# The inverse multiplied into the state's readers, the decay into its update rows, ahead of a recurrence's chain

## The chip, the cores and the metric

One core of a Trainium2 chip runs the whole program in one launch. The metric is the device time of that launch in microseconds, the median over several runs. Three runs of the kernel before took 2877.94, 2882.4 and 2890.2 us.

## The reference, cut to what matters

The program is two blocks of two layers each. The change is in the mixer of the first block, which runs twice (layer 0 with 512 tokens of output, layer 1 with 256). One of its branches is a recurrence over 512 tokens (8 chunks of 64), in 4 heads of 64 channels and 2 directions d, in float32:

```
def step(S, inp):                       # S: (G, H, dh, dh), one state per direction and head
    r_t, w_t, k_t, v_t, z_t, b_t = inp
    s_z = einsum('ghvk,ghk->ghv', S, z_t)
    S = S * w_t[:, :, None, :] + s_z[..., None] * b_t[:, :, None, :] + v_t[..., None] * k_t[:, :, None, :]
    return S, einsum('ghvk,ghk->ghv', S, r_t)
```

The other branches of the mixer, all of which the program interleaves with the recurrence, are a neighbourhood attention (q, k, v by projection, softmax, output), a 31-tap convolution, and the projection of a modulation vector.

## The kernel before, in words

The recurrence is computed chunk by chunk. Two heads share the 128 partitions (`halves`: rows o of one head, rows r of the other), `hp` counts the two pairs of heads, `u = (2d+hp)*8 + c` a chunk c of direction d. Its stages are generators: prep (p) makes ZR (slot 0 the readers of the state for s_z, slot 1 the readers for the output) and BK (the update rows b and k), both divided or multiplied by the running decay LAM; gram (g) makes the masked products S of BK with ZR for each chunk; inverse (i) inverts a unit triangular 64x64 matrix per chunk into TD, by a forward substitution on VectorE over 32x32 blocks (lines 681 to 698), four transposes TD and two TN (lines 704, 706) and two rounds of 32x32 products on TensorE (psinv); chain (c) carries the state PP through the chunks.

A chunk of the chain is three products one behind the other. First ZR[c,0] x PP plus S x UV (the v rows) into a bank, copied by VectorE to RH (line 802); then TD x RH, copied to the other half of UV (line 810); then BT x UV, to which PP is added and which is multiplied by the chunk's decay (lines 821 to 824). `ready(c+1)` prepares the next chunk inside the chain: it transposes the v rows (products with `cst`, vv and vr) and BK on TensorE, and ScalarE writes them as UV (line 776) and BT (line 785). The output product py (S x UV and ZR[c,1] x PP, alternating into one bank) is not needed by the next chunk; layer 1 makes it for the last four chunks alone.

The order of the stages is written out by hand in the strings SEQ (layer 0 `...ggggginNnniNNcactcccttat...`, layer 1 `...gggiiNnnncttcmmaa...`, with n and N the six projections of q, k, v, called near, psnap in the profile; a attention, t taps, m modulation); within it a list scheduler sets the order on each engine when the program is built. The strings are the same in both kernels. A float32 product leaves two MATMUL records in the profile, a product of the projections (fp32r) one. In a row `out<-in,in` the moving operand stands first.

Of the kernel before, what the change touches and what calls it, by code (L numbers as in the profile page):

```python
# [10 lines left out]
F32 = mybir.dt.float32  # L11
F32R = mybir.dt.float32r
I32 = mybir.dt.int32
AF = mybir.ActivationFunctionType
ALU = mybir.AluOpType
AX = mybir.AxisListType
PSUM = bass.MemoryType.PSUM
NOSYNC = mybir.DependencyInfo(mybir.DependencyClass.NoSync, mybir.DependencyReason.DATA)
# [122 lines left out]
class K:  # L141
    def __init__(self, tc, nc, A):
        self.tc, self.nc, self.A = tc, nc, A
        self.last = {}
        self.n = 0
        self.lab = ""

# [4 lines left out]

    def mm(self, out, lhsT, rhs, start, stop, chain=None, **kw):
        i = self.nc.tensor.matmul(out, lhsT, rhs, start=start, stop=stop, **kw)  # L154
        return self._chain(i, chain)

    def tp(self, out, in_, ident, chain=None):
# [302 lines left out]
    def mixer(self, l, x, b, X, M, need):  # L460

        tc, nc, A = self.tc, self.nc, self.A
# [96 lines left out]
        SS = ExitStack()  # L559
# [97 lines left out]
        def gram():  # L657
# [6 lines left out]
            for dh in range(4):  # L664
                for ab in range(2):
                    o = slice(64 * ab, 64 * ab + 64)
                    for c4 in range(2):
# [7 lines left out]
                                                self.gm[:, None, 128 * ab:128 * ab + 64 * z].to_broadcast([128, 4, 64 * z]), ALU.mult)  # L675
                        yield

        def inverse():

            with pool("PI", "right") as PI:  # L680
                Ad = PI.tile([128, 32, 32], F32, name=self.nm("Ad"), tag="Ad")
                Xi = PI.tile([128, 32, 32], F32, name=self.nm("Xi"))
                nc.sync.dma_start(Xi, A["cst"][:, C_X0:C_X0 + 1024].rearrange("p (a b) -> p a b", a=32))
                for g in range(4):
                    o, to = slice(32 * g, 32 * g + 32), 32 * (g % 2)
# [12 lines left out]
                        nc.vector.tensor_reduce(Xi[:, r, t:t + 1], w, AX.X, ALU.add)  # L698
                yield
                TN = PI.tile([128, 32, 32], F32, name=self.nm("TN"), tag="pd")  # L700
                Gs = PI.tile([128, 32, 32], F32, name=self.nm("Gs"), tag="Ad")
                for g in range(4):
                    o, to = slice(32 * g, 32 * g + 32), 32 * (g % 2)
                    nc.vector.transpose(TD[o, :, to:to + 32].rearrange("p u s -> p s u"), Xi[o].rearrange("p j s -> p s j"))
# [2 lines left out]
                for uh in range(2):  # L707
                    pg = self.ps((128, 16, 32))
                    for u in range(16):
                        for ab in range(2):  # L710
                            a, b = slice(64 * ab, 64 * ab + 32), slice(64 * ab + 32, 64 * ab + 64)
                            self.mm(pg[b, u], S[a, 1 - ab, uh * 16 + u, 32:64], TN[a, uh * 16 + u], True, True,
                                    tile_position=(64 * ab, 64 * ab + 32))
                    for ab in range(2):
                        b = slice(64 * ab + 32, 64 * ab + 64)
                        nc.scalar.copy(Gs[b, uh * 16:uh * 16 + 16], pg[b])
                    pt = self.ps((128, 16, 32))
                    for u in range(16):
                        for ab in range(2):
                            a, b = slice(64 * ab, 64 * ab + 32), slice(64 * ab + 32, 64 * ab + 64)  # L720
                            self.mm(pt[a, u], Gs[b, uh * 16 + u], TD[b, uh * 16 + u, 32:64], True, True,
                                    tile_position=(64 * ab + 32, 64 * ab))
                    for ab in range(2):
                        a = slice(64 * ab, 64 * ab + 32)
                        nc.scalar.copy(TD[a, uh * 16:uh * 16 + 16, 32:64], pt[a])
            yield

        def near():
# [32 lines left out]

        def chain():

            with pool("PC", "right", bufs=2) as PC:
                def ready(c):

                    UV = PC.tile([128, 2, 2, 2, 64], F32, tag="UV", name=self.nm("UV"))
                    pv = self.ps((128, 2, 2, 64), tag="x")
                    for d in range(2):
                        for hp in range(2):  # L770
                            for ab in range(2):
                                o = slice(64 * ab, 64 * ab + 64)
                                self.mm(pv[o, d, hp], (vr if d else vv)[o, hp, c * 64:c * 64 + 64], self.ident[o, o], True, True, chain=pv)
                    for ab in range(2):
                        o = slice(64 * ab, 64 * ab + 64)
                        nc.scalar.copy(UV[o, :, :, ab], pv[o])
                    if c == 7:
                        return UV, None
                    BT = PC.tile([128, 2, 2, 2, 64], F32, tag="BT", name=self.nm("BT"))
                    pb = self.ps((128, 2, 2, 128), tag="x")  # L780
                    for d in range(2):
                        for hp in range(2):
                            self.tp(pb[:, d, hp], BK[:, 2 * d + hp, c].rearrange("p a t -> p (a t)"), self.ident, chain=pb)
                    for ab in range(2):
                        nc.scalar.activation(BT[:, :, :, ab], pb[:, :, :, 64 * ab:64 * ab + 64], AF.Copy, scale=self.sg[:, ab:ab + 1])
                    return UV, BT

                halves = [(slice(64 * ab, 64 * ab + 64), slice(64 - 64 * ab, 128 - 64 * ab)) for ab in range(2)]
                PP = [None, None]
                UV, BT = ready(0)  # L790
                for c in range(8):
                    RH, Pn = [], [None, None]
                    for d in range(2):
                        pr = self.ps((128, 2, 64), tag=f"c{d}")
                        for hp in range(2):
                            u = (2 * d + hp) * 8 + c
                            for ab, (o, r) in enumerate(halves):
                                self.mm(pr[r, hp], S[o, ab, u, 0:64], UV[o, d, hp, ab], True, PP[d] is None, chain=pr)
                                if PP[d] is not None:
                                    self.mm(pr[r, hp], ZR[o, 2 * d + hp, c, 0], PP[d][o, hp], False, True, chain=pr)  # L800
                        RH.append(PC.tile([128, 2, 64], F32, tag=f"RH{d}", name=self.nm("RH")))
                        nc.vector.tensor_copy(RH[d], pr)
                    for d in range(2):
                        pu = self.ps((128, 2, 64), tag=f"c{d}")
                        for hp in range(2):
                            u = (2 * d + hp) * 8 + c
                            for ab, (o, r) in enumerate(halves):
                                self.mm(pu[r, hp], TD[r, u], RH[d][r, hp], True, True, chain=pu)
                        for ab, (o, r) in enumerate(halves):
                            nc.vector.tensor_copy(UV[r, d, :, ab], pu[r])  # L810
                    for d in range(2):
                        if c == 7:
                            break
                        pp = self.ps((128, 2, 64), tag=f"c{d}")
                        for hp in range(2):
                            for ab, (o, r) in enumerate(halves):
                                self.mm(pp[o, hp], BT[:, d, hp, ab], UV[:, d, hp, ab], True, True, chain=pp)
                        Pn[d] = PC.tile([128, 2, 64], F32, tag=f"PP{d}", name=self.nm("PP"))
                        lam = LAM[:, 2 * d:2 * d + 2, c, 64:65].to_broadcast([128, 2, 64])
                        if PP[d] is None:  # L820
                            nc.vector.tensor_tensor(Pn[d], pp, lam, ALU.mult)
                        else:
                            nc.vector.tensor_add(Pn[d], pp, PP[d])
                            nc.vector.tensor_tensor(Pn[d], Pn[d], lam, ALU.mult)
                    nxt = ready(c + 1) if c < 7 else None
                    if need or c >= 4:
                        py = self.ps((128, 2, 2, 64), tag="x")
                        for d in range(2):
                            for hp in range(2):
                                u = (2 * d + hp) * 8 + c  # L830
                                for ab, (o, r) in enumerate(halves):
                                    self.mm(py[o, d, hp], UV[:, d, hp, ab], S[:, ab, u, 64:128], True, PP[d] is None, chain=py)
                                    if PP[d] is not None:
                                        self.mm(py[o, d, hp], PP[d][o, hp], ZR[o, 2 * d + hp, c, 1], False, True, chain=py)
                        nc.scalar.copy(ZR[:, :, c, 1], py.rearrange("p d h t -> p (d h) t"))
                    PP = Pn
                    if nxt:
                        UV, BT = nxt
                        yield
            SS.close()  # L840

        def attend():
# [808 lines left out]
```

## Time and profile before

| | us |
|---|---|
| median of three runs | 2882.4 |
| the profiled run | 2886.99 |
| its span | 2885.2 |
| gram's end to chain's start, layer 0 | 169.8 to 260.4 |
| chain, layer 0 | 260.4 to 353 |
| gram's end to chain's start, layer 1 | 1009.1 to 1070.9 |
| chain, layer 1 | 1070.9 to 1154 |

The profile is of one execution. TensorE (PE) is busy for 95% of the span; its weight loads (PEld) run beside its products. The two mixers take some 90 to 445 us and 950 to 1200 us of the span; what lies behind them (feed-forward, experts, the second block) is not touched by the diff.

### The profile page before, as it was taken

The numbers are of one execution on the slowest core, as the hardware profiler recorded it, in microseconds if no ns is written. First come the engines' busy times: TensorE is split into PE (matmuls) and PEld (weight loads), VectorE is DVE, ScalarE is ACT, GpSimd is POOL, SyncE is SP. The second block draws the span as 40 slices with busy tenths as digits, with TensorE's granted clock in tenths as the row PEclk, the third lists the DMA queues.
The fourth block names the chain that finished last, engine by engine and source line by source line (L and its number), as shares of the span: only waits on it lengthen the run. The fifth ranks groups of instructions, "written<-read, shape, count | busy, mean of one in ns | idle before, by whom it ended". The sixth has DMA issues, their size and how long they took to land. (4 is left out here: it accounts for less than half of the span.)

```text
span 2885.2 us, 42860 instructions
## 1 busy us (share of the span) xinstructions
PE 2750.6 (95%) x17006; PEld 2257.8 (78%) x17006; DVE 1988.4 (69%) x2753; ACT 1468.3 (51%) x2032; POOL 348.5 (12%) x256
## 2 busy tenths in 40 slices
PE   6998999999998879999989999999999999999999
PEld 4677656778886766677867777778777889998999
DVE  4685474322225796488878888888889868856784
ACT  3313243322224332477757777767777646644563
POOL 1420012211001610100000000000000221301120
PEclk9898799999999998999999999999999999999999
DMA  6122155333333224579988999899989835553453
GB/s 227 51 74 74 52 150 193 96 123 94 97 99 105 81 88 140 173 293 352 319 321 325 322 353 344 328 338 362 337 325 349 307 114 175 183 183 117 161 184 109
DMA packets 108098, 585.77 MB, mean 203 GB/s; under 512 B 12657, under 2 KB 19825, under 8 KB 54129
## 3 DMA queue, kind: packets, MB, share of 16 engines
q1 hardware_dynamic: 107888, 582.95, 57.5%
q8 instruction: 136, 2.23, 0.3%
q14 instruction: 74, 0.60, 0.1%
HBM read 580.80 MB, written 2.10 MB: 202 GB/s over the span
## 5 line engine op out<-in xcount | busy, mean ns | idle before, releaser
L183 DVE TENSOR_TENSOR wl<-wr,wh 128x1024 fp32r<-128x1024 f32 x978 | 1169.5, 1225 | 477.9 <-ACT wh L182 465.6
L182 ACT CAST wh<-wr 128x1024 fp32r<-128x1024 f32 x992 | 1003.8, 1044 | 681.1 <-PE psffn L154 193.2
L154 PE MATMUL psmoe<-wh,xH 128*128 128x512 f32 x896 | 354.9, 397 | 3.4 <-ACT wh L182 3.4
L154 PE MATMUL psmoe<-wl,xH 128*128 128x512 f32 x896 | 356.2, 398 | 1.0 <-DVE wl L183 0.7
L154 PE MATMUL psmoe<-wh,xL 128*128 128x512 f32 x896 | 355.5, 397 | 0.0
L154 PEld LDWEIGHTS psmoe<-wl,xH 128*128 128x128 f32 x896 | 168.3, 188 | 45.6 <-DVE wl L183 6.5
L154 PEld LDWEIGHTS psmoe<-wh,xH 128*128 128x128 f32 x896 | 168.4, 188 | 44.4 <-ACT wh L182 5.0
L154 PE MATMUL pssf<-oh,wl 128*128 128x256 f32 x704 | 199.5, 284 | 0.0
L154 PE MATMUL pssf<-ohT,wh 128*128 128x256 f32 x704 | 199.2, 284 | 0.0
L154 PEld LDWEIGHTS psmoe<-wh,xL 128*128 128x128 f32 x896 | 168.4, 188 | 39.1
L154 PE MATMUL pssf<-oh,wh 128*128 128x256 f32 x704 | 198.9, 284 | 0.0
L154 PE MATMUL psmoe<-wh,aL 128*128 128x512 f32 x448 | 178.3, 398 | 2.0 <-DVE aL L183 2.0
L154 PE MATMUL psmoe<-wh,aH 128*128 128x512 f32 x448 | 175.6, 397 | 2.5 <-ACT aH L182 2.5
L154 PE MATMUL psmoe<-wl,aH 128*128 128x512 f32 x448 | 163.3, 400 | 0.0
L1551 POOL TENSOR_SCALAR x<-x,fin 128x256 f32<-128x256 f32 x8 | 12.2, 1542 | 1057.5 <-DMA wr<-w_in 1057.3
L154 PE MATMUL psffn<-h2L,wh 128*128 128x512 f32 x352 | 138.7, 394 | 1.3 <-POOL h2L L257 1.3
L154 PE MATMUL psffn<-h2H,wh 128*128 128x512 f32 x352 | 138.2, 395 | 1.0 <-ACT h2H L256 1.0
L154 PE MATMUL psffn<-h2H,wl 128*128 128x512 f32 x352 | 137.5, 392 | 0.0
L154 PEld LDWEIGHTS pssf<-oh,wl 128*128 128x128 f32 x704 | 135.2, 192 | 0.0
L154 PEld LDWEIGHTS pssf<-ohT,wh 128*128 128x128 f32 x704 | 135.1, 192 | 0.0
L154 PEld LDWEIGHTS pssf<-oh,wh 128*128 128x128 f32 x704 | 135.0, 192 | 0.0
L154 PEld LDWEIGHTS psmoe<-wh,aL 128*128 128x128 f32 x448 | 84.2, 188 | 24.4 <-DVE aL L183 4.4
(476 smaller groups left out, 5624.6 us busy)
## 6 DMA issues: line engine op xcount, KB each, us to landing
wr<-moe_w_gate SPq DMA_DIRECT2D x112, 1024.0 KB, 7.0
wr<-moe_w_up SPq DMA_DIRECT2D x112, 1024.0 KB, 6.6
wr<-moe_w_down SPq DMA_DIRECT2D x112, 1024.0 KB, 7.0
wm<-mod_w SPq DMA_DIRECT2D x96, 512.0 KB, 4.3
wr<-f_up SPq DMA_DIRECT2D x44, 1024.0 KB, 4.9
wr<-w_in SPq DMA_DIRECT2D x52, 512.0 KB, 3.8
wr<-w_in SPq DMA_DIRECT2D x16, 1024.0 KB, 5.0
wr<-f_down SPq DMA_DIRECT2D x16, 1024.0 KB, 5.0
```

The lines of the kernel that those rows point to most:

```text
L154: i = self.nc.tensor.matmul(out, lhsT, rhs, start=start, stop=stop, **kw)
L182: self.nc.scalar.copy(H, src)
L183: (eng or self.nc.vector).tensor_sub(L, src, H.bitcast(F32))
L1551: nc.gpsimd.tensor_scalar(x[:, k], x[:, k], fin[:, k:k + 1], None, op0=ALU.mult)
```

## The change

A new function `turned` runs at the head of the inverse stage. It does for all chunks what `ready` did in the chain: the v rows into UV and the products S x UV (now kept in the other half of UV), the transposes of BK. Ahead of the transpose ScalarE multiplies BK by the chunk's decay (28 instructions per layer, in place), and the result overwrites BK. It also transposes the readers ZR[c+1,0] (56 new products per layer). Behind the inverse, 56 more products per layer multiply TD into these readers (ZR again). The chain has ZR x PP, added onto TD x UV, copied to UV by VectorE, then BK x UV, to which PP times the decay (LP) is added. The buffers Ad, Xi and Gs of the inverse now lie in v, the tile of the attention's values. `self.after` in `mm` is never set.

```
+        def turned():
+            lam = PC.tile([128, 4, 8], F32, name=self.nm("lam"))
+            nc.vector.tensor_copy(lam, LAM[:, :, :, 64])
+            UV = LAM[:, :, :, 0:64], PC.tile([128, 4, 8, 64], F32, name=self.nm("UV"))
+            for c in range(8):
+                pv = self.ps((128, 2, 2, 2, 64))
+                for d in range(2):
+                    for hp in range(2):
+                        for o, r in halves:
+                            self.mm(pv[o, 0, d, hp], (vr if d else vv)[o, hp, c * 64:c * 64 + 64], self.ident[o, o], True, True, chain=pv)
+                for ab, (o, r) in enumerate(halves):
+                    nc.scalar.copy(UV[ab][o, :, c], pv[o, 0].rearrange("p d h t -> p (d h) t"))
...
+                            self.mm(pv[r, 1, d, hp], S[o, ab, (2 * d + hp) * 8 + c, 0:64], UV[ab][o, 2 * d + hp, c], True, True, chain=pv)
+                for ab, (o, r) in enumerate(halves):
+                    nc.scalar.copy(UV[ab][r, :, c], pv[r, 1].rearrange("p d h t -> p (d h) t"))
+                if c == 7:
+                    break
+                pb = self.ps((128, 4, 2, 64))
+                for dh in range(4):
+                    b = BK[:, dh, c].rearrange("p a t -> p (a t)")
+                    nc.scalar.activation(b, b, AF.Copy, scale=lam[:, dh, c:c + 1])
+                    self.tp(pb[:, dh].rearrange("p a t -> p (a t)"), b, self.ident, chain=pb)
+                for ab in range(2):
+                    nc.scalar.activation(BK[:, :, c, ab], pb[:, :, ab], AF.Copy, scale=self.sg[:, ab:ab + 1])
+            for dh in range(4):
+                pz = self.ps((128, 7, 64))
+                for c in range(7):
+                    for o, r in halves:
+                        self.mm(pz[r, c], ZR[o, dh, c + 1, 0], self.ident[o, o], True, True, chain=pz)
+                nc.scalar.copy(ZR[:, dh, 1:, 0], pz)
...
         def inverse():
+            turned()
...
+                Ad, Xi = [v[:, 2 * i:2 * i + 2]... for i in range(2)]
...
+                    for dh in range(2 * uh, 2 * uh + 2):
+                        pz = self.ps((128, 7, 64))
+                        for c in range(7):
+                            for o, r in halves:
+                                inverted = self.mm(pz[o, c], ZR[r, dh, c + 1, 0], TD[r, dh * 8 + c + 1], True, True, chain=pz)
+                        nc.vector.tensor_copy(ZR[:, dh, 1:, 0], pz)
...
+            def own(d, c):
+                W = self.ps((128, 2, 2, 64), tag=f"c{d}")
+                if c:
+                    for hp in range(2):
+                        for ab, (o, r) in enumerate(halves):
+                            self.mm(W[o, 0, hp], BK[:, 2 * d + hp, c - 1, ab], UV[ab][:, 2 * d + hp, c - 1], True, True, chain=W)
+                for hp in range(2):
+                    for ab, (o, r) in enumerate(halves):
+                        self.mm(W[r, 1, hp], TD[r, (2 * d + hp) * 8 + c], UV[ab][r, 2 * d + hp, c], hp == 0, c == 0 and hp == 1, chain=W)
+                return W
...
+            for c in range(8):
+                for d in range(2):
...
+                                self.mm(W[d][r, 1, hp], ZR[o, 2 * d + hp, c, 0], PP[d][o, hp], False, hp == 1, chain=W[d])
+                    for ab, (o, r) in enumerate(halves):
+                        nc.vector.tensor_copy(UV[ab][r, 2 * d:2 * d + 2, c], W[d][r, 1])
+                for d in range(2):
...
+                    W[d] = own(d, c + 1)
...
+                        nc.vector.tensor_add(Pn[d], W[d][:, 0], LP[d])
...
+                        nc.vector.tensor_tensor(LP[d], Pn[d], lam[:, 2 * d:2 * d + 2, c + 1:c + 2].to_broadcast([128, 2, 64]), ALU.mult)
```

Counted over the built program, per layer: TensorE gets 112 products of 64x64 more, all in the inverse stage, and 156 move there from the chain; ScalarE gets 32 copies of 64x256 where 16 were, 28 new scalings of 128x128 and 4 new copies of 128x448; VectorE loses the 16 copies RH and gets 4 copies of 128x448.

On TensorE, layer 0, at the end of gram. Before, the q projection follows:

```order
L154 MATMUL psgram_1120<-ZR_458,BK_462 128x128 x4
L154 MATMUL psgram_1126<-ZR_458,BK_462 128x128 x4
L154 MATMUL psnap_1277<-hH_235,wh_1267 128x512
L154 MATMUL psnap_1277<-hL_236,wh_1267 128x512
L154 MATMUL psnap_1277<-hH_235,wl_1268 128x512
```

In the changed kernel, at the same place:

```order
L162 MATMUL psinv_1159<-cst,BK_462 128x128 x4
L155 MATMUL psnap_1590<-hH_235,wh_1580 128x512
L155 MATMUL psnap_1590<-hL_236,wh_1580 128x512
L155 MATMUL psnap_1590<-hH_235,wl_1581 128x512
L155 MATMUL psinv_1170<-cst,vv_219 64x64 x4
L155 MATMUL psinv_1170<-cst,vr_220 64x64 x3
L155 MATMUL psinv_1138<-cst,vv_219 64x64 x4
```

Here turned (psinv) stands between gram and the projections. In all, 11 products psnap of layer 0 stand inside turned and 181 between turned and the inverse's own products; in layer 1 it is 9 and 73.

On ScalarE at that place (wh is a cast of weights for the projections), before:

```order
L182 CAST wh_1331<-wr_1329 128x1024
L732 ACTIVATE q_226<-psnap_1277 128x512
L182 CAST wh_1337<-wr_1335 128x1024
L732 ACTIVATE q_226<-psnap_1278 128x512
```

and in the changed kernel, the scalings of all seven chunks ahead of the first copies:

```order
L716 ACTIVATE BK_462<-BK_462,lam_1135 128x128 x4
L186 CAST wh_1586<-wr_1584 128x1024
L716 ACTIVATE BK_462<-BK_462,lam_1135 128x128 x24
L719 ACTIVATE BK_462<-psinv_1159,cst 128x4x64 x2
L702 COPY LAM_463<-psinv_1138 64x4x64
L702 COPY UV_1137<-psinv_1138 64x4x64
```

The 78 instructions of turned on ScalarE are followed by the next cast wh and the copies q; before, these came at once.

On TensorE, in one chunk of the chain of layer 0. Before (PE's order around the products TD x RH and BT x UV; psatt is the attention):

```order
L154 MATMUL pschain_2139<-RH_2126,TD_906 64x64 x4
L154 MATMUL pschain_2170<-cst,vv_219 64x64 x3
L154 MATMUL pschain_2146<-RH_2137,TD_906 64x64 x4
L154 MATMUL pschain_2153<-UV_2077,BT_2089 64x64 x4
L154 MATMUL psatt_2405<-PT_2403,v_228 64x128
L154 MATMUL pschain_2161<-UV_2077,BT_2089 64x64 x4
L158 MATMUL pschain_2182<-cst,BK_462 128x128 x4
```

(rows of the attention between them are left out). In the changed kernel a whole chunk reads, in pairs that repeat:

```order
L155 MATMUL pschain_2493<-LAM_463,BK_462 64x64
L155 MATMUL pschain_2493<-UV_1137,BK_462 64x64
L155 MATMUL pschain_2493<-LAM_463,TD_906 64x64
L155 MATMUL pschain_2493<-UV_1137,TD_906 64x64
L155 MATMUL pschain_2508<-S_905,LAM_463 64x64
L155 MATMUL pschain_2508<-ZR_458,PP_2435 64x64
L155 MATMUL pschain_2482<-PP_2491,ZR_458 64x64 x4
L155 MATMUL pschain_2493<-PP_2502,ZR_458 64x64 x4
L155 MATMUL psatt_2600<-PT_2598,v_228 64x128
```

Four products BK, four TD, for each direction; then the 16 of py (S and ZR in turn); then the eight ZR x PP of the next chunk, and the attention's products while VectorE copies.

## Rows read from the trace of the kernel before

**Rows 1.** The page, part 1: busy time and share of each engine

```profile
PE 2750.6 (95%) x17006; PEld 2257.8 (78%) x17006; DVE 1988.4 (69%) x2753; ACT 1468.3 (51%) x2032; POOL 348.5 (12%) x256
```

**Rows 2.** Stretches of layer 0: busy by engine, PEclk granted clock, DMA share

```profile
169.80:215.50 45.70, 44.06 (x193) 35.79 (x192) 45.54 (x130) 11.21 (x14) 10.76 (x4) 1.00 0.22 70
215.50:230.00 14.50, 4.46 (x131) 3.97 (x130) 14.36 (x9) 2.93 (x5) 0.00 (x0) 0.68 0.00 1
230.00:260.30 30.30, 30.30 (x320) 29.67 (x319) 4.32 (x4) 8.85 (x16) 0.00 (x0) 0.82 0.27 88
260.30:353.00 92.70, 91.68 (x1001) 65.48 (x999) 49.00 (x122) 26.23 (x64) 0.00 (x0) 0.80 0.20 64
```

**Rows 3.** The same columns, stretches of layer 1

```profile
1042.80:1063.50 20.70, 5.22 (x35) 4.93 (x34) 20.48 (x32) 1.59 (x3) 0.00 (x0) 0.67 0.04 14
1070.80:1154.00 83.20, 82.29 (x1029) 53.81 (x1028) 55.90 (x161) 26.50 (x66) 0.61 (x1) 0.91 0.52 159
```

**Rows 4.** Waits of PE, 169 to 260 us, then 1010 to 1071 us

```profile
PE psinv L154 <- DVE TN L706: 10.0, 2, 5.8
...
PE psinv L154 <- DVE TN L706: 15.5, 2, 14.3
```

**Rows 5.** Stretch of psnap alone, products of 128x256: busy, (x count)

```profile
246.00:256.00 10.00, 10.00 (x86) 10.00 (x85) 1.11 (x3) 1.00 0.34 107
```

**Rows 6.** Timeline of PE in layer 1: start, length, instruction [idle before]

```profile
1004.84 4.22 PE L154 MATMUL psgram<-ZR,BK 64*128 64x64 f32 x42
...
1063.49 2.21 PE L154 MATMUL psinv<-TN,S 32*32 32x32 f32 x124 [1.14 <-DVE TN L706]
...
1066.67 2.44 PE L154 MATMUL psinv<-TD,Gs 32*32 32x32 f32 x126
...
1070.87 0.45 PE L154 MATMUL pschain<-cst,vv 64*64 64x64 f32 x8
```

**Rows 7.** Groups of ScalarE instructions: shape, count, busy us, mean ns

```profile
L776 ACT COPY UV<-pschain 64x256 f32<-64x256 f32 x16 | 5.9, 366 | 9.5 <-PE pschain L154 8.2 <-DVE RH L802 1.2
L785 ACT ACTIVATE BT<-pschain,cst 128x256 f32<-128x256 f32 x14 | 5.9, 470 | 6.1 <-PE pschain L158 6.1
L835 ACT COPY ZR<-pschain 128x256 f32<-128x256 f32 x7 | 2.6, 372 | 31.1 <-PE pschain L154 31.1
L876 ACT COPY q<-psatt 128x128 f32<-128x128 f32 x3 | 0.8, 265 | 4.4 <-PE psatt L154 4.4
L410 ACT ACTIVATE xg<-x,G 128x256 f32<-128x256 f32 x8 | 4.0, 494 | 0.0
L1477 ACT ACTIVATE vt<-pssp,r 128x128 f32<-128x128 f32 x2 | 0.6, 362 | 0.0
```

**Rows 8.** Timeline of PE and ACT, first chunk of the chain, layer 0

```profile
260.38 0.45 PE L154 MATMUL pschain<-cst,vv 64*64 64x64 f32 x8
...
262.97 0.68 PE L154 MATMUL pschain<-UV,S 64*64 64x64 f32 x16
264.20 0.68 PE L154 MATMUL pschain<-RH,TD 64*64 64x64 f32 x16 [0.55 <-DVE RH L802]
...
266.98 0.66 PE L158 MATMUL pschain<-cst,BK 128*128 128x128 f32 x4
...
263.89 0.84 ACT L785 ACTIVATE BT<-pschain,cst 128x256 f32<-128x256 f32 x2
```

**Rows 9.** Timeline of PE, the output product py of one chunk, layer 0

```profile
311.13 0.33 PE L154 MATMUL pschain<-S,UV 128*64 128x64 f32 x2
311.39 0.32 PE L154 MATMUL pschain<-ZR,PP 64*64 64x64 f32 x2
...
312.93 0.47 PE L154 MATMUL pschain<-ZR,PP 64*64 64x64 f32 x2
313.34 0.47 PE L154 MATMUL pschain<-S,UV 128*64 128x64 f32 x2
```

**Rows 10.** Groups of VectorE, chain of layer 0: count, busy, mean ns, idle before

```profile
L802 DVE COPY RH<-pschain 128x128 f32<-128x128 f32 x16 | 4.5, 289 | 27.0 <-PE pschain L154 27.0
```

More of the change, by code (lines that the diff above doesn't have):

```diff
@@ L144, in __init__ @@
         self.last = {}
+        self.after = None
         self.n = 0
@@ L154, in mm @@
         i = self.nc.tensor.matmul(out, lhsT, rhs, start=start, stop=stop, **kw)
+        if self.after is not None:
+            self.tc.add_manual_dep(i.ins, self.after, NOSYNC, reason="the order of two stages")
+            self.after = None
         return self._chain(i, chain)
@@ L676, in gram @@
                         yield
+        halves = [(slice(64 * ab, 64 * ab + 64), slice(64 - 64 * ab, 128 - 64 * ab)) for ab in range(2)]
+        UV = PC = lam = inverted = None
+        def turned():
+            nonlocal UV, PC, lam
+            PC = SS.enter_context(pool("PC", "right"))
+            lam = PC.tile([128, 4, 8], F32, name=self.nm("lam"))
[30 more added lines that the diff above has]
+                nc.scalar.copy(ZR[:, dh, 1:, 0], pz)
@@ L678, in inverse @@
         def inverse():
+            nonlocal inverted
+            turned()
             with pool("PI", "right") as PI:
-                Ad = PI.tile([128, 32, 32], F32, name=self.nm("Ad"), tag="Ad")
-                Xi = PI.tile([128, 32, 32], F32, name=self.nm("Xi"))
+                Ad, Xi = [v[:, 2 * i:2 * i + 2].rearrange("p a b -> p (a b)").rearrange("p (a b) -> p a b", a=32) for i in range(2)]
                 nc.sync.dma_start(Xi, A["cst"][:, C_X0:C_X0 + 1024].rearrange("p (a b) -> p a b", a=32))
@@ L700, in inverse @@
                 TN = PI.tile([128, 32, 32], F32, name=self.nm("TN"), tag="pd")
-                Gs = PI.tile([128, 32, 32], F32, name=self.nm("Gs"), tag="Ad")
+                Gs = Ad
                 for g in range(4):
@@ L762, in chain @@
         def chain():
[L764 to L768, printed above, removed]
-                    for d in range(2):
[L770 to L794, printed above, removed]
@@ new lines, in own @@
+            def own(d, c):
[4 more added lines that the diff above has]
+                            self.mm(W[o, 0, hp], BK[:, 2 * d + hp, c - 1, ab], UV[ab][:, 2 * d + hp, c - 1], True, True, chain=W)
+                for hp in range(2):
+                    for ab, (o, r) in enumerate(halves):
+                        self.mm(W[r, 1, hp], TD[r, (2 * d + hp) * 8 + c], UV[ab][r, 2 * d + hp, c], hp == 0, c == 0 and hp == 1, chain=W)
+                return W
@@ new lines, in chain @@
+            PP, LP = [None, None], [None, None]
+            W = [own(d, 0) for d in range(2)]
+            for c in range(8):
+                Pn = [None, None]
+                for d in range(2):
+                    if PP[d] is not None:
+                        for hp in range(2):
+                            for o, r in halves:
+                                self.mm(W[d][r, 1, hp], ZR[o, 2 * d + hp, c, 0], PP[d][o, hp], False, hp == 1, chain=W[d])
+                    for ab, (o, r) in enumerate(halves):
+                        nc.vector.tensor_copy(UV[ab][r, 2 * d:2 * d + 2, c], W[d][r, 1])
+                for d in range(2):
+                    if c == 7:
+                        break
+                    W[d] = own(d, c + 1)
+                    Pn[d] = PC.tile([128, 2, 64], F32, tag=f"PP{d}", name=self.nm("PP"), bufs=2)
+                    if LP[d] is None:
+                        nc.vector.tensor_copy(Pn[d], W[d][:, 0])
+                    else:
+                        nc.vector.tensor_add(Pn[d], W[d][:, 0], LP[d])
+                for d in range(2):
+                    if c < 6:
+                        LP[d] = PC.tile([128, 2, 64], F32, tag=f"LP{d}", name=self.nm("LP"))
+                        nc.vector.tensor_tensor(LP[d], Pn[d], lam[:, 2 * d:2 * d + 2, c + 1:c + 2].to_broadcast([128, 2, 64]), ALU.mult)
+                if need or c >= 4:
+                    py = self.ps((128, 2, 2, 64), tag="x")
+                    for d in range(2):
@@ L797, in chain @@
                             for ab, (o, r) in enumerate(halves):
-                                self.mm(pr[r, hp], S[o, ab, u, 0:64], UV[o, d, hp, ab], True, PP[d] is None, chain=pr)
+                                self.mm(py[o, d, hp], UV[ab][:, 2 * d + hp, c], S[:, ab, u, 64:128], True, PP[d] is None, chain=py)
                                 if PP[d] is not None:
-                                    self.mm(pr[r, hp], ZR[o, 2 * d + hp, c, 0], PP[d][o, hp], False, True, chain=pr)
-                        RH.append(PC.tile([128, 2, 64], F32, tag=f"RH{d}", name=self.nm("RH")))
@@ L802, in chain @@
[L802 to L839, printed above, removed]
+                                    self.mm(py[o, d, hp], PP[d][o, hp], ZR[o, 2 * d + hp, c, 1], False, True, chain=py)
+                    nc.scalar.copy(ZR[:, :, c, 1], py.rearrange("p d h t -> p (d h) t"))
+                PP = Pn
+                if c < 7:
+                    yield
             SS.close()
```

## The prediction, made before the changed kernel was timed

> **What bounds the kernel now.** I read the busy shares first, then the stretches of the two mixers, then TensorE's waits, then the timeline of single stages. TensorE is the engine to watch: busy for 95% of the span [rows 1]. The change touches two stretches in each layer. In the first, from gram's end to the chain, VectorE sets the pace: its forward substitution and transposes keep it busy for 45.5 of 45.7 us and 14.4 of 14.5 us, and TensorE, out of projections to do, waits 10.0 us in layer 0 and 15.5 us in layer 1 for the transposes TN [rows 2, 4]; there it has 4.46 us of work in 14.5 us, then 5.22 us in 20.7 us [rows 2, 3]. In the second, the chain, TensorE is busy for 91.7 of 92.7 us and 82.3 of 83.2 us [rows 2, 3], because attention, taps and modulation fill in; the granted clock there is 0.80 and 0.91 on the mean of its two levels. VectorE has 49 us of work in the chain of layer 0 and waits 27.0 us for TensorE before the copies RH [rows 10]. So the chain is limited by what TensorE has to issue, not by the length of the recurrence. A shorter recurrence pays only by the TensorE time that leaves the stretch, and work put ahead of the chain is free only in the 10 and 15.5 us of waiting.
>
> **The change, part by part: the head of the inverse.** All of `turned` stands on TensorE between gram and nearly all the projections (11 products psnap inside it in layer 0, 9 in layer 1). ScalarE paces it. Per layer: 32 copies of 64x256 at 0.366 us, 11.7 us; 14 sign changes at 0.470 us, 6.6 us; 28 scalings of 128x128, for which no row has the same form: the copy of 128x128 takes 0.265 us, the 128x256 one with a scale 0.494 us, and the 128x128 one with a scale out of PSUM 0.362 us; I take 0.36, the nearest form, so 10.1 us (7.4 to 13.8); 4 copies of 128x448, by the step from 0.265 us at 128 to 0.372 us at 256 about 0.53 us each, 2.1 us [rows 7]. That is 30.5 us. A weight cast stands among them, 1.0 us; handing over between the engines I put at 2 us (0 to 15, see the second rival); TensorE is free again before the last three copies end, -1.5 us. Turned takes 32 us. TensorE's own part is smaller: 184 products of two records at 29 ns, 10.7 us (eight records more make 0.23 us, 16 against 8 in [rows 8]), and 28 transposes, some 3 us. So it idles for about half of turned, and after such a stretch the clock has been at its lower level here (mean 0.68, then 0.82, around the 10 us wait [rows 2]); I add 2.5 us for about 5 us of projections at half speed.
>
> Layer 0: gram ends at 169.8, turned at 201.8. 181 projections of 128x512 at 0.228 us (193 in 44.06 us [rows 2]) are 41.3 us, with the 2.5 us: 245.6. VectorE's transposes are over before that (its stretch ended by 230), so the wait of 10 us is gone. The inverse's own products take 2.2 and 2.4 us at full clock [rows 6], rounded together to 4.7; the new 56 products TD x readers are 112 records, 3.2 us; the 192 projections of v at 0.116 us (86 in 10.0 us [rows 5]), 22.3 us. The chain starts at 275.8 instead of 260.4 [rows 8]: 15.4 us later.
> Layer 1: gram ends at 1009.1, turned at 1041.0; 62 projections of 128x512 and 11 of 128x256 with the 2.5 us end at 1058.9, 28 more at 1062.1; the second TN comes at 1063.5 as before [rows 6]; 4.7, 3.2 and 153 x 0.116 = 17.8 us follow: 1089.2 instead of 1070.9, 18.3 us later. Before, all but 46 of these projections lay in VectorE's shadow; now turned lies there, and is paid for by the projections that come out behind it. Together: +33.7 us.
>
> The other edits of this stage I cost at nothing. VectorE's 4 copies of 128x448 lie beside the last 148 and 113 projections. That Ad, Xi and Gs lie in v makes the v copies of layer 1 wait for the inverse's last products; these come before the 113 projections that need the banks. If that cover went, a copy of some 0.4 us for each of four banks would show.
>
> **The chain.** What leaves it per layer: the v and S x UV products, 128 instructions, 256 records at 29 ns, 7.4 us; 28 transposes, 0.11 us each without the tail of the last (four in 0.66 us [rows 8]), 3.1 us. What it costs to change the shape in which the array is used shows in py: the 128x64 and 64x64 products alternate there at 0.257 us a pair of records instead of 0.058, so a change is 0.20 us [rows 9]. A chunk before has three such changes ahead of py (into BT, into the transposes, back), one after the change has five (BK, TD, BK, TD, py): +2 x 7 x 0.20 = 2.8 us against it. py itself, 16 changes per chunk, stays. Net 7.7 us at full clock; at 0.80 and 0.91 that is 9.6 and 8.5 us. The Trainium skill, "TensorEngine Tiling (Array Packing)", Key Properties, says that changing the tiling mode, not just the tile, drains the engine. The trace agrees (0.257 against 0.058 us), and by it the rule speaks against the new order of BK and TD; left out, the chain would gain 7 us more over the two layers.
> The hop over RH goes: a copy of 0.289 us and the wait around it, seen bare once (0.55 us idle [rows 8]), otherwise beside other products. I take the copy once per chunk, 2.3 us a layer (0 to 4.4). The two VectorE steps of the decay shrink to one addition; they lay beside py and were worth nothing. The chain gives back 9.6 + 8.5 + 4.6 = 22.7 us.
>
> **Sum.** +33.7 - 22.7 = +11.0 us. The profiled run took 2886.99 us, so it would take 2898.0; the median of the runs before is 4.6 us lower, 2882.4, and the predicted median is 2893 us.
>
> **Rivals.**
> *Turned is a chain of its own, slower.* Each chunk goes TensorE, ScalarE, TensorE, ScalarE, and only three banks serve it. The first `ready` before, which has two of its steps, took from 260.38 to 264.73 us with 1.5 us of other ScalarE work in it [rows 8]: 2.8 us. With the second pair of copies, the second product and the scalings a chunk is 5.7 us; eight unoverlapped, 46 us, and the last copies 2: 48 us. Three banks let some overlap; at 42 us instead of 32 it is +20 us, 2913. It decides once turned lasts about 40 us. For it: ScalarE has strict turns between flips and copies of different chunks. Against: the 28 scalings run in one piece ahead of everything, and the scheduler puts three chunks of v side by side.
> *The chain is a latency chain after all, faster.* If the whole hop (0.29 + 0.55 us) counts in all 16 chunks, the chain gives 13.4 instead of 4.6 us for it; and if the scalings are at 0.265 us, the clock holds, and handing over costs nothing, the starts come 14 us earlier: 33.7 - 14 - 31.5 = -12 us, 2870. For it: the 27.0 us that VectorE waits for RH. Against: 98 to 99% of the chain is TensorE at work.
> *The products only change places.* Then the added 112 products a layer (6.5 us) are hidden in the vanished waits, turned and chain cancel: 2882. It is the low end of the forecast, and I count it there.
>
> **Chances and range.** The forecast (2880 to 2905) has 0.52, the slow turned 0.23, the faster chain 0.25. A difference of 0.5% (14.4 us: below 2868 or above 2896.8) is about what a measurement of this kernel can tell from no change. Of the forecast 0.33 lie within it and 0.19 above; the slow turned is all above; of the faster chain half, 0.13, is beyond it, 0.12 within. Faster 0.13, same 0.45, slower 0.42. The range reaches to both rivals: 2868 to 2918; the forecast's own is 2880 to 2905.
>
> **What would show it.** Right, if: TensorE's wait for TN is gone in layer 0 and below 5 us in layer 1; the stretch of psinv before the projections is 29 to 36 us with ScalarE busy for over 85% of it and TensorE for about half; the chains start near 276 and 1089 us and last about 81 and 72 us; py still alternates at about 0.26 us. Wrong, if turned is much shorter or longer than 32 us, if the scalings of BK are far from 0.36 us, if psnap begins well inside turned, or if the chain shortens by more than 16 us in a layer while TensorE stays full.

## The result, and the profile after

The kernel after takes 2905.2 us (median of 12 runs, 2885.2 to 2918.8), the kernel before 2882.6 us (median of 12): ratio 1.0071, interval 1.0049 to 1.0092. It is slower by 0.7%. The forecast was 2893 in 2868 to 2918. The profiled run took 2905.42 us, 18.4 us more than the one before. One of the twelve runs of the kernel with layer 0 alone new, further down, fell in a slower state of the chip and is left out of its figures.

The first step in reading it is to keep two things apart: how long the program takes in TensorE's own cycles, and at what clock it runs. The runs of one kernel differ by over 1% in time, but the span multiplied by its mean granted clock hardly differs: of after 2799.8 to 2806.5 us, mean 2803.2 ± 1.4 (95%). Below this product is called the work; it counts waits too, and by half where the clock is at its lower level. For a whole kernel over its runs it is a good measure, for one stretch a rougher one: the chain of layer 0 in its form of before comes to 74.2 us at a clock of 0.80 [rows 2] and to 78.6 us at 1.00 (last row of this document). Before has 2783.5 ± 1.0 (35 runs). So the change adds **19.7 ± 1.7 us of work**, at the same mean clock (0.9658, before 0.9656).

Part 1 of the page after (busy us by engine, [rows 1] of before): TensorE is busy for 28.6 us more.

```profile
PE 2779.2 (96%) x17454; PEld 2269.1 (78%) x17454; DVE 1975.4 (68%) x2731; ACT 1500.3 (52%) x2128; POOL 345.2 (12%) x256
```

The stretches of layer 0 after: head with turned, projections in VectorE's shadow, the rest up to the chain, chain, and what lies behind it up to the end of the mixer's output projection (columns as in [rows 2]: stretch, length, busy of PE, PEld, DVE, ACT, POOL, granted clock, DMA share and GB/s).

```profile
171.80:196.00 24.20, 22.84 (x415) 18.45 (x415) 24.07 (x99) 19.46 (x53) 0.00 (x0) 1.00 0.01 3
196.00:240.00 44.00, 39.89 (x169) 32.56 (x168) 27.98 (x39) 11.22 (x14) 9.60 (x4) 0.96 0.23 74
240.00:274.30 34.30, 34.30 (x568) 32.45 (x566) 7.40 (x8) 11.80 (x20) 0.00 (x0) 1.00 0.24 75
274.30:351.70 77.40, 77.40 (x706) 52.89 (x708) 37.02 (x93) 14.04 (x32) 0.00 (x0) 0.74 0.19 62
351.70:510.50 158.80, 152.06 (x838) 89.99 (x842) 90.12 (x184) 57.62 (x136) 26.71 (x23) 0.89 0.45 143
```

Turned alone, from its first product to the last that turns ZR, in layer 0 and in layer 1:

```profile
171.80:194.30 22.50, 21.14 (x408) 17.03 (x407) 22.37 (x93) 18.93 (x52) 0.00 (x0) 1.00 0.01 3
1025.80:1047.10 21.30, 20.31 (x406) 16.15 (x406) 21.18 (x88) 18.79 (x52) 0.00 (x0) 1.00 0.01 3
```

The last of the stretches of layer 0 in the kernel before, which the rows ahead of the prediction don't show:

```profile
353.00:492.90 139.90, 135.89 (x827) 84.13 (x826) 81.25 (x171) 56.69 (x134) 26.90 (x23) 0.97 0.48 155
```

Layer 1, head, chain and what is behind it, after; then the same three of before:

```profile
1025.80:1103.90 78.10, 69.93 (x1027) 61.33 (x1027) 55.58 (x138) 34.89 (x78) 12.06 (x5) 0.93 0.14 42
1103.90:1174.60 70.70, 69.11 (x739) 42.25 (x742) 45.53 (x130) 15.69 (x38) 0.61 (x1) 0.93 0.56 172
1174.60:1245.80 71.20, 68.32 (x519) 48.37 (x520) 40.00 (x93) 31.93 (x70) 12.70 (x15) 0.95 0.59 194
```

```profile
1009.10:1070.80 61.70, 46.18 (x519) 41.99 (x519) 57.42 (x134) 15.49 (x25) 12.64 (x5) 0.89 0.17 52
1070.80:1154.00 83.20, 82.29 (x1029) 53.81 (x1028) 55.90 (x161) 26.50 (x66) 0.61 (x1) 0.91 0.52 159
1154.00:1226.90 72.90, 69.08 (x512) 50.06 (x513) 34.41 (x78) 32.43 (x72) 12.60 (x15) 0.92 0.54 175
```

In time, layer 0 loses 12.0 us ahead of the chain, gains 15.3 in it and loses 18.9 behind it (+15.6); layer 1 loses 16.4, gains 12.5 and 1.7 (+2.2). Multiplied by the clock of each stretch, the two layers look alike: layer 0 +20.3, -16.9, +5.6, that is +9.0 us of work; layer 1 +17.7, -10.0, +0.6, that is +8.3. The difference is the clock: it was at its lower level in the waits ahead of the chain before (0.68 and 0.82 [rows 2]); after, the head runs at 1.00 and the chain (0.74) and the stretch behind it (0.89) are lower. The profile of one execution can't say whether that belongs to the change; the experiments ask.

Two lists of waits of TensorE, layer 0 and then layer 1 (who waits, for whom, us, times, longest). The 10.0 us for TN [rows 4] are gone; in their place 4.1 us stand for the split weights wl, which VectorE makes between steps of its substitution (last two lines). In layer 1, 7.2 of 15.5 us are left.

```profile
PE psnap L155 <- DVE wl L187: 4.1, 1, 4.1
...
PE psinv L155 <- DVE TN L759: 7.2, 1, 7.2
...
206.74 1.21 DVE L187 TENSOR_TENSOR wl<-wr,wh 128x1024 fp32r<-128x1024 f32 x1
208.01 0.50 PE L155 MATMUL psnap<-hH,wl 128*128 128x512 f32 x1 [4.11 <-DVE wl L187]
```

ScalarE's groups in turned (155 to 200 us; count, busy us, mean ns, idle before). The scalings (L716) occupy 8.7 us. They started from 156.5 us on as gram freed each block, and all but the last few lay beside gram, which ended at 171.8.

```profile
L716 ACT ACTIVATE BK<-BK,lam 128x128 f32<-128x128 f32 x28 | 8.7, 388 | 2.3 <-PE psgram L155 2.3
L719 ACT ACTIVATE BK<-psinv,cst 128x256 f32<-128x256 f32 x14 | 5.8, 466 | 0.1
...
L702 ACT COPY UV<-psinv 64x256 f32<-64x256 f32 x8 | 2.9, 368 | 0.1
...
L727 ACT COPY ZR<-psinv 128x448 f32<-128x448 f32 x4 | 2.0, 530 | 0.6 <-PE psinv L155 0.6
```

### The profile page after: what moved, and what is told of

Read it like the earlier page. It is cut to its first block, busy times and chain, and to the rows that moved or that the text cites. A ratio compares the mean times of both kernels' runs of the same rounds, so it can differ in the third digit from the quotient of the medians.

```text
span 2903.6 us, 43848 instructions
## 1 busy us (share of the span) xinstructions
PE 2779.2 (96%) x17454; PEld 2269.1 (78%) x17454; DVE 1975.4 (68%) x2731; ACT 1500.3 (52%) x2128; POOL 345.2 (12%) x256
```

## The experiments

Theory: the change costs TensorE work, in either layer, because the chain was bound by what TensorE issues. Rivals: the loss is the clock behind the chain of layer 0; or the chain is bound by its hops and the loss is turned's ScalarE work.

**One layer at a time.** Both forms of the two functions stand in the kernel:

```
-  "i": inverse(), "n": near(), "c": chain()
+  "i": (inverse if l == 0 else inverse0)(), ..., "c": (chain if l == 0 else chain0)()     # l == 1 in the other
```

Layer 0 alone new. 

> Only layer 0 has the new form, layer 1 is as before. Work theory: the change costs TensorE work, about the same in either layer. Counted at full clock (span x mean granted clock) before is 2784.2 us and after 2804.9; of the +20.7 the stretch of the mixer shows +8.9 in layer 0 (290.6 to 299.5) and +9.1 in layer 1 (207.9 to 217.0). So this kernel takes 9 to 12 us more than before (+0.3 to +0.4%), and its span x clock is about 2794. Clock theory: what is lost is lower clock behind the chain of layer 0, where the profiled run is 15.7 us longer (323.0 to 338.7 us from gram's end to swout's end) against some 2 us in layer 1. Then this kernel takes 16 to 20 us more than before, nearly the whole loss.

Layer 1 alone new. 

> Only layer 1 has the new form, layer 0 is as before. Work theory: 9 to 12 us more than before, span x clock about 2794. Clock theory: 1 to 4 us more than before, which can hardly be told from none.

Measured: layer 0 alone 2902.0 us, ratio 1.0055 (1.003 to 1.008), work 2792.5 ± 1.9; layer 1 alone 2886.8 us, ratio 1.0018 (0.9993 to 1.0043), work 2793.1 ± 1.8. In work the work theory holds: both are within 2 us of the 2794 that it named, +9.0 and +9.6, together 18.6 of 19.7. In time the clock theory named the medians better (some 17 and 2 us more than before). But the two intervals overlap, and so do the mean clocks (0.9637 ± 0.0030 and 0.9670 ± 0.0025, before 0.9656 ± 0.0010), so it is not shown that layer 0 costs more time than layer 1. Nor is the low clock behind the chain of layer 0 shown to belong to the change: with the same form there, the profiled run of layer 0 alone new has a clock of 0.98 in that stretch, where after has 0.89, and the stretch is 145.1 us long instead of 158.8. Length times clock is some 6 us more than before, as in after.

```profile
341.43:486.52 145.09, 138.94 (x835) 85.09 (x836) 89.98 (x184) 57.55 (x135) 26.74 (x23) 0.98 0.47 156
```

**The fold left out.** The two loops over `pz` go (turning ZR, TD x ZR):

```
-  self.mm(pz[r, c], ZR[o, dh, c + 1, 0], self.ident[o, o], True, True, chain=pz)
-  inverted = self.mm(pz[o, c], ZR[r, dh, c + 1, 0], TD[r, dh * 8 + c + 1], True, True, chain=pz)
```

> The 112 products a layer that turn the readers ZR and multiply TD into them are left out with their 8 copies; the chain still has its two products per chunk, so its recurrence computes something else. Work theory: these products stand bare on TensorE, 4.21 + 3.56 us in layer 0 and 4.04 + 3.56 in layer 1, so the kernel takes 15.4 us less than after, 2888 to 2892, still 5 to 8 us more than before. Cover theory (they lie in what VectorE needs for the substitution and in ScalarE's time, as the prediction's third rival has it): 0 to 5 us less than after, above 2899.

Measured: 2894.4 us, ratio 1.0029 (1.0008 to 1.005); work 2792.0 ± 1.4, 11.2 ± 1.9 less than after. Between the two: the products are dear, but not all of their 15.4 us were bare. Without them TensorE idles more ahead of the chain; in layer 0 the length less PE's busy time is 9.2 us, against 5.5 after (102.5 - 97.0).

```profile
171.48:269.53 98.05, 88.84 (x926) 76.07 (x925) 56.99 (x141) 40.55 (x84) 9.58 (x4) 0.97 0.19 60
269.53:343.28 73.75, 73.75 (x703) 50.20 (x702) 37.01 (x93) 13.91 (x32) 0.00 (x0) 0.79 0.20 65
343.28:492.74 149.46, 140.76 (x836) 87.41 (x836) 90.09 (x184) 57.40 (x135) 26.70 (x23) 0.97 0.48 152
```

**Moved, not folded.** Besides, the chain gets its third product back:

```
+  self.mm(pr[r, hp], ZR[o, 2 * d + hp, c, 0], PP[d][o, hp], True, True, chain=pr)
+  nc.vector.tensor_add(RH[d][r], pr[r], UV[ab][r, 2 * d:2 * d + 2, c])
+  self.mm(pu[r, hp], TD[r, (2 * d + hp) * 8 + c], RH[d][r, hp], True, True, chain=pu)
```

> The computation is whole. Everything is moved ahead of the chain as in after (v rows, S x UV, BK scaled and transposed), but TD is not multiplied into the readers: the chain has three products per chunk again, ZR x PP, an addition on VectorE to RH, TD x RH. Work theory: the chain is bound by TensorE's work, the extra hop lies beside attention and modulation, so this kernel is within 4 us of the one without the fold (about 2890), 15 us faster than after, and 4 to 10 us slower than before. Latency theory: the hop over RH counts in all 16 chunks, 16 x (0.29 + 0.55) = 13.4 us, so it is 13 us slower than the one without the fold and level with after.

Measured: 2889.1 us, ratio 1.0009 (0.9988 to 1.003); work 2801.9 ± 1.5, clock 0.9708. By its work the latency theory comes nearer: the hop costs 9.9 ± 2.0 us of the 13.4 it named. By its time the other one does (16.0 us below after), because this kernel was granted more clock than the one without the fold (0.9654); why it was is not shown. The hop here is not quite that of before: it has 28 additions to RH per layer where before has 16 copies. The stretches show where it is paid: the chain of layer 0 takes 81.0 us instead of 73.75, though TensorE idles in it for 2.3 us only: 40 records of attention and modulation more are let in (743 against 703). They are missing behind it (796 against 836), and yet that stretch is no shorter: TensorE idles there for 9.8 us, without the third product for 8.7. In the chain of layer 1 the profiled runs show no such price. The rows: ahead of the chain, chain and behind it in layer 0; the chain of layer 1; the chain of layer 1 in the kernel without the fold.

```profile
171.75:269.82 98.07, 88.87 (x926) 76.04 (x925) 57.00 (x141) 40.60 (x84) 9.61 (x4) 0.97 0.19 60
269.82:350.84 81.02, 78.72 (x743) 50.53 (x742) 44.87 (x122) 15.09 (x35) 0.00 (x0) 0.79 0.28 92
350.84:500.14 149.30, 139.52 (x796) 86.60 (x796) 89.70 (x183) 56.61 (x132) 26.54 (x23) 0.97 0.42 134
1086.98:1154.47 67.49, 66.12 (x756) 39.83 (x756) 49.06 (x147) 17.29 (x40) 0.61 (x1) 1.00 0.61 193
...
1079.37:1148.39 69.02, 66.52 (x739) 40.89 (x742) 45.52 (x130) 15.67 (x37) 0.61 (x1) 0.98 0.55 176
```

These two give the change in three parts, in work: moving v, S x UV and BK ahead of the chain +18.4 (2783.5 to 2801.9), dropping the hop (in the form it has here) -9.9, paid for by the fold, +11.2.

**py in two groups.** All S x UV of a chunk, then all ZR x PP, in the same bank (in after; the same in before):

```
-  for d, hp, ab:  py += UV x S;  py += PP x ZR
+  for d, hp, ab:  mm(py[o, d, hp], UV[ab][..], S[:, ab, u, 64:128], (d, hp) == (0, 0), PP[d] is None and (d, hp) == (1, 1))
+  for d, hp, ab:  mm(py[o, d, hp], PP[d][o, hp], ZR[o, 2 * d + hp, c, 1], False, (d, hp) == (1, 1))
```

Before with it. 

> The kernel before, with py in two groups per chunk: first its eight products S x UV (128x64), then its eight ZR x PP (64x64), instead of alternating. Shape-change theory: each of the 14 changes that go costs 0.20 us in each of the 11 chunks that alternate (7 in layer 0, 4 in layer 1), 30.8 us. Span x clock falls from 2783.5 to about 2753, the median from 2885 to about 2853 if the clock stays at 0.966. Load theory: a 128x64 product is dear by itself (its weights), and the order changes nothing: 2780 to 2790. Clock theory: the work goes, but the denser chain is granted a lower clock (below 0.963), and half of the gain is lost: about 2867.

After with it. 

> The kernel after, with the same grouping of py. Work theory: the same 30.8 us go as from before, so it stays 20 us slower than the kernel before with py grouped: span x clock 2772, median about 2873. Latency theory: with 2.8 us less filler in a chunk the chain is bound by its hops, and the change, which takes one hop out of three, now pays: this kernel comes within 8 us of the kernel before with py grouped, or below it.

After with it, and own in two groups:

```
-  W[d] = own(d, c + 1)          # BK, TD of one direction, then of the other
+  W = own(c + 1)                # BK of both, then TD of both
```

> As the one before it, and own() issues BK of both directions and then TD of both (BK BK TD TD, not BK TD BK TD). Shape-change theory: two changes less in each of 14 chunks, 14 x 2 x 0.20 = 5.6 us off its span x clock (about 2766). If a wait takes their place, since the second direction's W must be free before the first TD: no change, or up to 4 us more.

Moved, not folded, with it. 

> All of turned but the fold, three products per chunk in the chain, and py grouped. Work theory: 30.8 us less than the same kernel with py alternating (span x clock 2801.9): 2771, median about 2857. Latency theory: the moved form showed 9.9 us of span x clock more than the form without the fold, by its hop; with less filler the hop stands bare and the gain is 15 to 20 us only: about 2784, and the folded form (the one with py grouped alone) is the faster of the two.

| py grouped in | median us | ratio to before | work | mean clock |
|---|---|---|---|---|
| before | 2832.5 | 0.9839 (0.9815 to 0.9863) | 2757.3 ± 1.9 | 0.9732 |
| after | 2847.9 | 0.9894 (0.9864 to 0.9925) | 2780.2 ± 2.9 | 0.9760 |
| after, own grouped | 2849.8 | 0.9913 (0.9881 to 0.9945) | 2780.4 ± 2.1 | 0.9750 |
| moved, not folded | 2848.7 | 0.9892 (0.9865 to 0.9919) | 2773.1 ± 5.4 | 0.9738 |

(Before beside them: 2877.4 us, work 2785.0 ± 2.7, clock 0.9679.) The kernel before with py grouped beats both kernels of this study, by 1.6% and some 2.3% (0.9839 / 1.0071). Its py in the timeline of TensorE; before it alternated at 0.257 us a pair [rows 9], and after too:

```profile
299.49 0.69 PE L154 MATMUL pschain<-S,UV 128*64 128x64 f32 x16
```

```profile
320.15 0.47 PE L155 MATMUL pschain<-S,UV 128*64 128x64 f32 x2
320.56 0.47 PE L155 MATMUL pschain<-ZR,PP 64*64 64x64 f32 x2
...
329.19 0.32 PE L155 MATMUL pschain<-ZR,PP 64*64 64x64 f32 x2
329.44 0.33 PE L155 MATMUL pschain<-S,UV 128*64 128x64 f32 x2
```

Sixteen records are started as one run of 0.69 us; alternating, two take 0.41 us at half clock and 0.25 us at full. The shape-change theory named 30.8 us, the work fell by 27.7 in before and 23.0 in after: right for the most part, and the order of products, the same in number and kind, is worth more than the whole change. The load theory falls. Another reading is left: in a pair, one product adds onto what the other has just written. The chain before has this with a single shape, S x UV and then ZR x PP, both 64x64, and there four records take 0.12 us, the 0.058 a pair of a run; so the adding is not what is dear.

```profile
267.85 0.33 PE L154 MATMUL pschain<-UV,S 64*64 64x64 f32 x4
267.96 0.33 PE L154 MATMUL pschain<-PP,ZR 64*64 64x64 f32 x4
268.08 0.33 PE L154 MATMUL pschain<-UV,S 64*64 64x64 f32 x4
```

The clock theory falls the other way round: the clock rose. The two chains of before with py grouped, then those of after with it:

```profile
261.98:320.99 59.01, 57.84 (x1002) 41.42 (x1002) 48.51 (x122) 26.85 (x65) 0.00 (x0) 1.00 0.28 92
1041.18:1107.22 66.04, 64.98 (x1031) 42.34 (x1030) 54.71 (x160) 26.32 (x66) 0.89 (x1) 1.00 0.61 194
```

```profile
275.10:318.89 43.79, 43.75 (x711) 30.18 (x710) 36.74 (x94) 14.21 (x32) 0.00 (x0) 1.00 0.35 114
1057.34:1113.97 56.63, 55.13 (x744) 33.22 (x743) 46.09 (x131) 15.87 (x37) 0.61 (x1) 1.00 0.71 224
```

All four at 1.00, where the alternating chains had 0.80, 0.91, 0.74 and 0.93. The chain of layer 0 falls from 92.7 to 59.0 us without the change and from 77.4 to 43.8 with it. On this base the change costs 22.9 us of work and 15.4 us of time. That is nearer the work theory's 20 us than the latency theory's 8, though the figures that the work theory named for after (2772 and 2873 us) were missed by 8 and 25 us. The moved form comes out where the work theory had it (2771), and not at the latency theory's 2784: its work is 7.1 ± 5.6 us below the folded form's, and the medians are level. Its hop is still paid in the chain of layer 0, 48.9 us long where the folded form's is 43.8; by the work of the whole, the fold takes more than that elsewhere.

```profile
267.53:316.42 48.89, 45.59 (x743) 29.68 (x742) 44.37 (x122) 15.38 (x35) 0.00 (x0) 1.00 0.44 142
```

Grouping own changes nothing that the runs can tell (+0.2 ± 3.2 us of work): the chain of layer 0 gets 1.9 us shorter (43.79 to 41.87), that of layer 1 1.4 us longer. The first record of each group in a chunk shows what a change costs here: a group of eight products takes 0.61 us to the start of the next, where eight pairs at 0.058 us take 0.46, so 0.15 us and not 0.20. By that the edit would save 4.2 us and not 5.6; that it saves any is not shown.

```profile
271.21:313.08 41.87, 41.72 (x710) 29.21 (x710) 35.74 (x93) 14.01 (x32) 0.00 (x0) 1.00 0.37 128
1055.23:1113.22 57.99, 55.59 (x743) 33.93 (x743) 45.70 (x131) 15.77 (x37) 0.61 (x1) 0.97 0.69 219
...
291.26 0.27 PE L155 MATMUL pschain<-LAM,BK 128*64 128x64 f32 x1
291.88 0.27 PE L155 MATMUL pschain<-LAM,TD 64*64 64x64 f32 x1
292.49 0.27 PE L155 MATMUL pschain<-S,LAM 128*64 128x64 f32 x1
```

**Scalings doubled** (after):

```
+  nc.scalar.activation(b, b, AF.Copy, scale=1.0)
   nc.scalar.activation(b, b, AF.Copy, scale=lam[:, dh, c:c + 1])
```

> The kernel after, with each of the 28 scalings of BK per layer preceded by a copy of the same block in place: 28 x 0.307 = 8.6 us of ScalarE more per layer, and nothing more on TensorE. ScalarE theory (the prediction's: ScalarE paces turned, 30.5 us of its work on the path): turned grows by 8.6 us in either layer, the kernel by 17 us, span x clock about 2820, median about 2921. TensorE theory (the scalings lie beside gram, and turned is TensorE's own 18 us with projections in its gaps): span x clock stays at 2803 to 2807, the median within 5 us of after.

Measured: 2911.9 us, ratio to before 1.0092 (1.0058 to 1.0125); work 2801.5 ± 2.4, as after. The median is 6.7 us above after's, by a clock of 0.9637; work is what the edit could add, and it added none. Most of ScalarE's extra work lies beside gram; 14 and 16 of the 56 scalings and copies of a layer start behind gram's end (2 in after). In layer 0 all but one of them run at once there, and turned takes 23.1 us instead of 22.5. In layer 1 they are strewn over turned, which takes 24.9 us instead of 21.3, with ScalarE busy for 23.9 of them. Yet the chain starts no later behind gram's end than in after (102.4 us, after 102.5; layer 1 77.2, after 78.1), for TensorE's wait for TN in layer 1 is 5.0 us instead of 7.2. Turned in either layer, then from gram's end to the chain in either layer, then that wait:

```profile
168.20:191.30 23.10, 21.68 (x409) 17.12 (x409) 22.98 (x95) 21.40 (x64) 0.00 (x0) 1.00 0.01 3
1021.95:1046.90 24.95, 24.35 (x418) 18.34 (x418) 24.83 (x101) 23.89 (x68) 0.00 (x0) 1.00 0.01 2
168.20:270.59 102.39, 97.25 (x1149) 83.28 (x1149) 59.43 (x145) 44.94 (x100) 9.60 (x4) 0.98 0.18 58
1021.95:1099.11 77.16, 71.53 (x1028) 61.60 (x1028) 54.12 (x138) 38.35 (x92) 12.48 (x5) 0.96 0.13 43
...
PE psinv L155 <- DVE TN L760: 5.0, 1, 5.0
```

## Why the prediction was right, and where it was not

The direction of the argument held: TensorE bounds the chain, the work put ahead of it makes it start later, and the shorter recurrence gives back less than that. The forecast was 12 us low; the time lies at the upper end of its own range (2880 to 2905), and slower by more than 0.5% had a chance of 0.42, no difference 0.45.

That the sum came so near is in part luck. In the profiled runs the two chains start 28.2 us later (forecast 33.7) and give back 27.8 us (forecast 22.7). With these the sum would be +0.4 us and not +11.0. Nearly all that makes the profiled run longer lies behind the chains (+18.9 and -1.7 us), where the sum has nothing. In work the same three terms are +38.0, -26.9 and +6.2 us. Step by step:

- **Turned: "ScalarE paces it", 32 us, TensorE idle "for about half of turned".** Ten us too long. Turned takes 22.5 us in layer 0 and 21.3 us in layer 1, with TensorE busy for 21.1 and 20.3. The term that failed is the scalings, 10.1 us of the sum (measured 8.7): they lay beside gram, which the prediction had overlooked, and without them its sum is 21.9 us. That TensorE idles for half of it failed too. That ScalarE paces what is left is not refuted: it is busy for 18.9 and 18.8 us of turned, and in layer 1, where doubled scalings fell into turned, turned grew by 3.6 us. TensorE's part was put at 13.7 us; from each record's start to the next the v rows take 5.4 us, S x UV 4.9, BK 3.3 and the turning of ZR 4.2, together 17.8, waits for ScalarE among them.
- **The starts of the chains, 15.4 and 18.3 us later.** Measured, less what each layer was late at gram's end (2.0 and 16.7 us), 11.9 and 16.3: near, but the causes in the sum were not the ones. The wait for wl in the place of that for TN was not seen coming, and the wait in layer 1 stayed at 7.2 us instead of below 5.
- **The fold.** The 56 products TD x readers were put at 3.2 us and take 3.56; the turning was counted among what ScalarE hides. Both together take 7.8 us in layer 0 and stand mostly bare: without them the kernel has 11.2 us less work, of 15.4 in both layers.
- **The chain gives back 9.6 and 8.5 us, and 2.3 us each for the hop.** Measured 15.3 and 12.5 us. The products that leave were put at 10.5 us a layer at full clock; from each record's start to the next, times the clock, they take 15.5 us in the chain of layer 0 before and 14.4 in that of layer 1, waits and changes of shape among them. The hop is mis-sized too: 4.6 us for both layers, measured 9.9 in the form of the moved kernel. So far the second rival was true, and the fold eats it.
- **What lies behind the chain was taken as unchanged.** This is the step that made the forecast low. Layer 0 lost 5.6 us of work there (10 records of attention and modulation that found no room in the shorter chain, and idling), and some 6 with layer 0 alone new. The other 13 of the 18.9 us in the profile are clock, 0.97 to 0.89, which the run with layer 0 alone new does not repeat; they are not shown to belong to the change.
- **The change of shape, 0.20 us, with the Trainium skill's "TensorEngine Tiling (Array Packing)", Key Properties.** Confirmed where the order alternates product by product: 27.7 of 30.8 us in before, 23.0 in after. Between groups the trace shows 0.15 us a change, and own grouped moved the work by +0.2 ± 3.2 us, so the 2.8 us a layer that the prediction charged for it are not shown.
- **The rivals.** Slow turned: no, 22.5 us. Faster chain: in the chain itself more than half, 27.8 us between the forecast's 22.7 and its 31.5; but the starts came 5.5 us earlier than forecast and not 14, the fold took what the hop gave, and the stretch behind was added. Products only change places: no, moving alone adds 18.4 us of work. That they were the filler in which the chain's hops were hidden would explain it and is not shown by itself.

Open is where the 18.4 us come from. The moved products take 13.6 and 14.1 us in turned, no more than in the chain. In layer 0 the moved form has 14.7 us of work more than before ahead of the chain, 10.2 less in it and 9.1 more behind it; no run separates the causes.

## What to carry to other kernels

Where the bounding engine is 99% busy, a step less in the recurrence is worth less than its length: here the hop gave back 9.9 us, and the products added to drop it took 11.2. Before restructuring such a chain, look in its timeline for the same products in a costlier order, here two shapes alternating at four times the price of a run of one. Compare versions by span times granted clock as well as by time: a difference of 0.3% was plain in the first and inside the interval of the second. What is moved out of a chain has to be looked for in every stage, those behind the chain too.

## What the runs showed of the hardware

A busy TensorE is no assurance of the higher clock. In the chains of before and after of layer 0 its records leave hardly a gap (91.7 of 92.7 and 77.4 of 77.4 us), and yet the clock stood at 1.2 GHz, the lower of its two levels, for 37 and 40 us of them (length x (1 - clock) x 2); before it fell there, TensorE had alternated between the two shapes of py, without a wait. With py grouped, no chain of the four kernels showed more than 3.4 us of it. But of the 14 profiled chains that alternate, two ran at 1.00 throughout: that of layer 1 in the moved form (67.49 us, row above), and that of layer 0 in the kernel with layer 1 alone new:

```profile
263.37:341.94 78.57, 77.01 (x1000) 54.49 (x999) 48.70 (x122) 26.21 (x64) 0.00 (x0) 1.00 0.24 75
```

In one execution of the moved form with py grouped the low clock came behind the chain (161.5 us at 0.87). So the order went with the clock in most of these profiles, and what decides it is not shown. The Trainium skill, "TensorE: Matmul & The Clock Gate", HAM oscillation, tells of a clock that falls while TensorE waits for data; here it fell in stretches without a recorded wait, and the page's case does not cover that.
